# Stick-breaking attention in a Conformer block: the third part's turns behind the next scores, the output's low part in place, the last pair's turns and some out-weight splits further back

## The chip, the cores and the metric

One Trainium2 chip (trn2), one of its cores. The metric is the device time of one execution in microseconds (us), as the median of several. The engines are named as in the profile: PE is TensorE (PEld its weight loads), DVE is VectorE, ACT is ScalarE, POOL is GpSimd, SP is SyncE, which here only issues DMAs. Each engine works through its own queue in order; an instruction that waits holds everything behind it on that engine.

## The reference

One Conformer layer on 1024 frames of width 1024, in float32:

```
x = x + 0.5 * swiglu(rms_norm(x, n1), wi1, wo1)
x = x + stick_breaking_attention(rms_norm(x, mix_norm), w_qkv, q_gain, k_gain, w_o)
x = x + 0.5 * swiglu(rms_norm(x, n2), wi2, wo2)
```

The attention has 16 heads of 64. With z = q.k/8 and strictly earlier frames s < t, the weight of frame s for frame t is sigmoid(z[t,s]) times the product of sigmoid(-z[t,j]) over the frames j between them. The values are summed with these weights, and the heads' outputs go through w_o.

## The kernel before

Every float32 product is made of three products of a high and a low part (`fp32r`): high by high, high by low, low by high. Making the two parts of a tile is called a **split** (`split`, lines 195 to 197): ACT copies the high part, then DVE or POOL subtracts it to get the low part. The kernel runs the first feed-forward block, the attention, the out-projection with w_o, and the second feed-forward block. The change lies in the attention and the out-projection alone.

**The attention** goes through eight pairs of heads, p = 0 to 7. A pair has four parts, a, b, c and d, with lengths in a plan's own units (`PARTS`, line 39). In each part three kinds of work are interleaved:

- *scores* of one head and one half of the frames (`UNITS`, line 41; function `scores`, from line 1038). For a block of 128 frames PE multiplies q and k into a bank `bz` (line 1058; three such banks), ACT takes two sigmoids of it (line 1062, into a tile `w` and back into the bank), DVE runs the product along the row (line 1066, into `om` or `w`), and POOL multiplies the two (line 1073, after a memset of one column, line 1071). The result is a row of attention weights in `w`. Head h and block i have the tile `w{h}{i}`, so `w03` is the last block of head 0.
- *turns and products with the values* of scores made a part earlier (`BEFORE`, line 42; function `values`, from line 1077). A *turn* is up to four transposes of 128x128 by PE into a bank `bt` (line 1095; two such banks), split into `th` and `tl` by ACT and DVE (line 1098). A *product* multiplies `th` and then `tl` into the bank `bo` (line 1113, called `apply` in the code). After the last product of a head ACT and DVE add the outcome to a tile `o` (lines 1118 and 1119), and after the second head of the pair `o` is itself split. For all pairs but the last the two parts went to the tiles `w12` and `w13`, and from there by DMA to DRAM (`o_keep`, lines 1120 to 1127); `load_o` (line 1134) brings them back into `xh` and `xl` for the out-projection. The last pair's parts are written to `xh` and `xl` directly.
- *fills*: the products of the next pair's q, k and v (lines 308 to 310 into the banks `bq`, 24 steps a pair, of six or nine matmuls of 128x384). With the last of a half come sums of squares on ACT and DVE (`sq`, `ssq`), then a chain of small DVE operations for an inverse root (lines 207 to 212), then the scaling of k on POOL (lines 996 and 999). `rs_a` on ACT (line 207) is the first link of that chain and waits for `ssq` (DVE, line 986).

**What sets the order.** Each step is put into a plan at a time in the plan's units: scores evenly over the part, fills evenly, the turns of a part from `TURN` = 4.0 on, and each product `APPLY` = 2.3 after its turn (lines 1187 to 1202). The steps are then emitted in the order of these times (line 1231), and a scheduler under the language reorders single instructions by priority and by what it thinks is ready. So each engine's order is fixed when the kernel is built. `sooner(n)` (line 153) raises the priority of what is emitted in it by n places, and `following(mark)` (line 192) lets an instruction be issued only after a marked one.

**The out-projection.** `out_weights` (line 1245) loads two of the eight row blocks of w_o for one half of the columns, and splits them: high part on ACT, low part on DVE, or on POOL if the name stands in `ON_POOL` (line 35). The first half's four pieces are split during pairs 6 and 7 (low parts: three on POOL, the fourth, tiles `wb` and `wc`, on DVE). The second half's first two pieces (`we`, `wf` and `wg`, `wh`) are split by ACT and DVE during the last pair, and its last two afterwards. As the last pair has no following pair, its fills are replaced by the out-projection's products for the first half of the columns (`SHARES`, line 49; `project`, line 1260), which need 128x512 matmuls of lines 308 to 310 with `raw`, `wa` to `wd` as weights.

Of the kernel before, what the change touches and what calls it, by code (L numbers as in the profile page):

```python
# [17 lines left out]
P = 128  # L18
T = 1024
# [12 lines left out]

BANKS = {"bz": 3, "bq": 2, "bt": 2, "bo": 1, "ka": 2, "kc": 2, "kb": 4, "ma": 4, "mb": 4}

ON_POOL = {"wo0", "wo1", "wo2"}

# [16 lines left out]
)  # L53

TURN, APPLY = 4.0, 2.3
RAW = 6
RH = 4
H_TILES = 8
# [55 lines left out]
def macaron_kernel(ctx, tc, x, g1, w1_in, w1_out, gm, w_qkv, gq, gk, w_o, g2, w2_in, w2_out, out):  # L114
# [801 lines left out]
    with ExitStack() as stack:  # L916
# [121 lines left out]
        def scores(state, hd, half):  # L1038

            w = state["w", hd, half] = {}  # L1040

            def step(tb, kb):
                L = T - tb * P
                if kb == half:
                    t = pl["w"].tile([P, T - tb % 4 * P], F32, name=f"w{hd}{tb % 4}", bufs=1)

                    om = t[:, L : 2 * L] if half else pl["om"].tile([P, T], F32, name="om")
                    state["om"], w[tb] = om, t[:, :L]
                om, wt = state["om"], w[tb]
                q = state["q", hd, half][:, (tb % 4) * P : (tb % 4 + 1) * P]  # L1050
                s0 = max(tb * P, kb * NHALF)
                n = (kb + 1) * NHALF - s0
                c0 = s0 - tb * P
                off = P if n == P else 0
                z = bank("bz")
                keys = slice(s0 - off - kb * NHALF, NHALF)
                for i in range(2):
                    pe.matmul(z[:, : off + n], q, state["k", hd, kb][i][:, keys], start=i == 0, stop=i == 1)  # L1058

                z = z[:, off : off + n]  # L1060
                for to, sign in ((wt[:, c0 : c0 + n], 0), (z, 1)):
                    marks["scored"] = act.activation(  # L1062
                        to, z, AF.Sigmoid, scale=state["f", half][:, sign, tb % 4, hd : hd + 1]
                    ).ins
                least = first[:, P : P + 1].to_broadcast([P, n]) if c0 else first[:, :n]
                dve.tensor_tensor_scan(  # L1066
                    om[:, c0 : c0 + n], z, least, initial=om[:, c0 - 1 : c0] if c0 else 0.0,
                    op0=ALU.mult, op1=ALU.max,
                )
                if c0 == 0:  # L1070
                    pool_e.memset(wt[:, 0:1], 0.0)
                c1 = max(c0, 1)
                pool_e.tensor_tensor(wt[:, c1 : c0 + n], wt[:, c1 : c0 + n], om[:, c1 - 1 : c0 + n - 1], op=ALU.mult)  # L1073

            return [partial(step, tb, kb) for tb in range(half * 4, half * 4 + 4) for kb in range(half, 2)]

        def values(state, p, hd, half):

            own, other = slice(hd * DH, (hd + 1) * DH), slice((1 - hd) * DH, (2 - hd) * DH)
            tb0 = half * 4  # L1080
            now = {}

            def blocks(sb):
                return min(4, sb - tb0 + 1)

            def turn(sbs):
                w = state["w", hd, half]
                tp = bank("bt")
                n = 0
                for sb in sbs:  # L1090
                    for i in range(max(blocks(sb), 2)):
                        c = (sb - tb0 - i) * P

                        src = w[tb0 + i][:, c : c + P] if i < blocks(sb) else first[:, P : 2 * P]
                        pe.transpose(tp[:, n : n + P], src, ident)
                        n += P
                th, tl = now[sbs] = [pl["th"].tile([P, NHALF], F32R, name=n) for n in ("th", "tl")]
                split(tp[:, :n], th[:, :n], tl[:, :n])

            def apply(sbs):  # L1100
                if hd == 0 and sbs[0] == NT - 1:
                    state["o", half] = pl["o"].tile([P, NHALF], F32, name=f"o{half}", bufs=1)
                if sbs[0] == NT - 1:
                    now["o"] = bank("bo")
                ot = now["o"]
                c = 0
                ts = now.pop(sbs)
                for sb in sbs:
                    n = max(blocks(sb), 2) * P
                    vv = state["v"][:, sb, 2 * hd : 2 * hd + 2, :].rearrange("p a b -> p (a b)")  # L1110
                    for i, t in enumerate(ts):
                        start, stop = sb == NT - 1 and i == 0, sb == tb0 and i == 1
                        pe.matmul(ot[:, :n], vv, t[:, c : c + n], start=start, stop=stop)  # L1113
                    c += n
                if sbs[-1] > tb0:
                    return
                o = state["o", half]
                act.activation(o[own, :], ot[other, :], AF.Copy)
                dve.tensor_tensor(o[own, :], ot[own, :], o[own, :], op=ALU.add)
                if hd == 1 and p < NP - 1:  # L1120

                    oh, ol = (
                        pl["w"].tile([P, T - i * P], F32R, name=f"w1{i}", bufs=1)[:, :NHALF] for i in (2, 3)
                    )
                    split(o, oh, ol)
                    for to, src in zip(o_keep, (oh, ol)):
                        sp.dma_start(to[rows(p), HALVES[half]], src.bitcast(F32))
                elif hd == 1:
                    split(o, xh[:, p, HALVES[half]], xl[:, p, HALVES[half]])

            groups = [(sb,) for sb in range(NT - 1, tb0 + 1, -1)] + [(tb0 + 1, tb0)]
            return [(partial(turn, sbs), partial(apply, sbs)) for sbs in groups]

        def load_o(half):

            for i in range(NP - 1):
                for to, src in zip((xh, xl), o_keep):
                    sp.dma_start(to[:, i, HALVES[half]].bitcast(F32), src[rows(i), HALVES[half]])


        states = [{} for _ in range(NP)]
        plan = []
# [34 lines left out]
        for p in range(-1, NP):  # L1177
# [9 lines left out]
            for part, span in PARTS.items():  # L1187
# [3 lines left out]
                if this is not None:  # L1191
                    groups = values(this, p, *BEFORE[part])
                    for i, (to_turn, to_apply) in enumerate(groups):
                        t = TURN + (span - TURN) * i / len(groups)
                        put(part, t, to_turn)
                        put(part, t + APPLY, to_apply)
            if nxt is not None:
                if p >= 0:
                    fills = qkv(p + 1, nxt)
                    for part, span in PARTS.items():  # L1200
                        for i in range(FILLS[part]):
                            put(part, (span - (3.0 if part == "d" else 0.0)) * (i + 0.5) / FILLS[part], fills.pop(0))
                put("c", 15.0, partial(prep_q, nxt, 1))
                put("c", 17.5 if p >= 0 else 20.0, partial(prep_k, nxt, 0, 1))
                put("d", 8.0, partial(prep_k, nxt, 1, 1))
# [35 lines left out]
    with pools(*PROJECTION) as pl:  # L1241
# [3 lines left out]
        def out_weights(c, k, rooms):  # L1245
# [7 lines left out]
            if c is HALVES[0] and k < 6:  # L1253

                there = seen[:, k // 2 : k // 2 + 1] if k < 4 else wo[-1][1][:, 0:1].bitcast(F32)
                pool_e.tensor_tensor((l_ if k < 4 else h_)[:, 0:1], there, there, op=ALU.mult)
            split(raw, h_, l_, lane(f"wo{k // 2}") if c is HALVES[0] else dve)
            return [(h_[:, s], l_[:, s]) for s in HALVES]

        def project(tb, ks, h, tags):  # L1260
# [106 lines left out]
```

## Time and profile before

| what | value |
| --- | --- |
| median of 3 runs | 1930.62 us (1930.38 to 1931.1) |
| profiled execution: its own time | 1931.22 us |
| profiled execution: span of its instructions | 1929.4 us |
| PE busy | 1906.1 us (99%) |
| DVE, POOL, ACT busy | 1237.0 us (64%), 1115.7 us (58%), 978.5 us (51%) |
| attention and the first half of the out-projection | about 667 to 1238 us of the span |

The profile shows one execution. A row of a timeline has the start in us from the span's first instruction, the length in us, the engine, the line, the operation, the tiles (out<-in), the shape and a count of merged neighbours. In brackets stands how long the engine had been idle and what ended that. Matmuls overlap: the next one starts before the one before has ended, so the cost of a matmul in a row of them is the distance from start to start. A wait is therefore a little longer than the idle time in brackets. The view of waits adds this idle time up by who waited for whom.

### The profile page before, as it was taken

Reading aid. Unit: us, or ns where it says so; the run is one execution under the profiler, and the core shown is the slowest. Engines: PE = TensorE matmul, PEld = TensorE weight load, DVE = VectorE, ACT = ScalarE, POOL = GpSimd, SP = SyncE. Lnnn points to the kernel's source line nnn. Section 1 sums busy time; section 2 is a strip of 40 time slices with the busy share of each in tenths; the row PEclk is TensorE's granted clock in tenths of the full one; section 3 lists DMA queues with packets and bytes.
Section 4 is the critical chain, followed back from the end, with each engine's and each line's share of the span. In section 5 each row is a group of like instructions: output and inputs, shape, how many; then the busy total and the mean of one; then the engine's idle time right before and its main releaser. Section 6 shows DMA issues by size and latency. Waiting matters only on the chain.

```text
span 1929.4 us, 26653 instructions
## 1 busy us (share of the span) xinstructions
PE 1906.1 (99%) x9362; PEld 1623.1 (84%) x9362; DVE 1237.0 (64%) x1714; ACT 978.5 (51%) x1794; POOL 1115.7 (58%) x994
## 2 busy tenths in 40 slices
PE   9999999999999999999999999999999999999999
PEld 8878888888888899898989897788888888888887
DVE  6855455536775667887787778477455545548645
ACT  6433433343335467777787777344433443334332
POOL 5766667656456646655665564114667667655554
PEclk9999999999999999999999999999999999999999
DMA  6233323238996401111101144511323323369973
GB/s 202 88 120 105 104 87 126 94 118 294 347 321 234 134 25 45 39 39 45 45 31 48 50 143 141 197 55 59 116 88 125 100 97 104 121 212 341 336 268 139
DMA packets 169558, 259.70 MB, mean 135 GB/s; under 512 B 11728, under 2 KB 82384, under 8 KB 169424
## 3 DMA queue, kind: packets, MB, share of 16 engines
q1 hardware_dynamic: 169280, 258.00, 39.2%
q8 instruction: 73, 1.20, 0.3%
q14 instruction: 61, 0.50, 0.1%
q10 hardware_dynamic: 144, 0.00, 0.0%
HBM read 197.66 MB, written 60.29 MB: 134 GB/s over the span
## 4 chain that ended last, share of the span: by engine, by line
PE 85%; DVE 7%; ACT 2%; POOL 2%; issue 2%; DMA 1%; SPq 0%; DVEq 0%; POOLq 0%; ACTq 0%
PE ka L308 6%; PE ka L310 6%; PE ka L309 6%; PE kc L308 4%; PE kc L310 4%; PE kc L309 4%; PE bq L309 4%; PE bq L308 4%; PE bq L310 4%; PE kb L308 4%; PE ma L309 4%; PE ma L310 4%; PE kb L310 4%; PE ma L308 4%; PE kb L309 4%; PE bo L1113 3%
## 5 line engine op out<-in xcount | busy, mean ns | idle before, releaser
L197 POOL TENSOR_TENSOR rp<-raw,rp 128x1024 fp32r<-128x1024 f32 x84 | 212.5, 2534 | 169.9 <-ACT rp L196 159.1
L197 POOL TENSOR_TENSOR u<-sf,u 128x512 fp32r<-128x512 f32 x160 | 227.4, 1423 | 136.4 <-ACT u L196 136.4
L197 POOL TENSOR_TENSOR u<-raw,u 128x512 fp32r<-128x512 f32 x128 | 186.2, 1457 | 157.9 <-ACT u L196 157.1
L196 ACT ACTIVATE u<-sf 128x512 fp32r<-128x512 f32 x160 | 100.8, 630 | 204.9 <-PE kb L309 86.9
L1073 POOL TENSOR_TENSOR w<-w,om 128x512 f32<-128x512 f32 (+4 forms) x128 | 140.8, 1104 | 110.2 <-DVE om L1066 83.9
L446 DVE TENSOR_TENSOR h<-h 128x512 f32<-128x512 f32 x110 | 135.4, 1235 | 85.7 <-POOL h L554 85.0
L196 ACT ACTIVATE rp<-rh 128x1024 fp32r<-128x1024 f32 (+1 forms) x78 | 76.5, 984 | 196.6 <-PE mb L309 59.2
L308 PE MATMUL bq<-wqh,xh 128*128 128x384 f32 x512 | 174.5, 341 | 0.0
L310 PE MATMUL bq<-wqh,xl 128*128 128x384 f32 x512 | 172.2, 336 | 0.0
L309 PE MATMUL bq<-wql,xh 128*128 128x384 f32 x512 | 172.0, 336 | 0.0
L576 DVE TENSOR_TENSOR raw<-raw 128x1024 f32<-128x1024 f32 (+1 forms) x60 | 89.9, 1500 | 109.8 <-DMA raw<-w_out 94.9
L196 ACT ACTIVATE u<-raw 128x512 fp32r<-128x512 f32 x128 | 80.3, 630 | 151.6 <-PE ka L309 100.9
L308 PE MATMUL ka<-xh,u 128*128 128x512 f32 x352 | 137.2, 390 | 1.9 <-ACT s L499 1.9
L308 PE MATMUL ma<-rp 128*128 128x512 f32 x352 | 137.0, 389 | 0.0
L310 PE MATMUL ka<-xh,u 128*128 128x512 f32 x352 | 137.0, 389 | 0.0
L310 PE MATMUL ma<-rp 128*128 128x512 f32 x352 | 136.9, 389 | 0.0
L309 PE MATMUL ka<-xl,u 128*128 128x512 f32 x352 | 136.9, 389 | 0.0
L309 PE MATMUL ma<-rp 128*128 128x512 f32 x352 | 136.9, 389 | 0.0
L1062 ACT ACTIVATE w<-bz,f 128x512 f32<-128x512 f32 (+2 forms) x192 | 112.7, 587 | 42.2 <-PE bz L1058 39.4
L554 POOL TENSOR_TENSOR h<-h,g 128x512 f32<-128x512 f32 x80 | 112.9, 1411 | 35.4 <-DVE h L503 33.6
L475 DVE TENSOR_TENSOR sf<-raw 128x512 f32<-128x512 f32 x80 | 80.3, 1003 | 77.9 <-POOL u L197 77.9
L197 DVE TENSOR_TENSOR rp<-rh,rp 128x1024 fp32r<-128x1024 f32 (+1 forms) x70 | 110.8, 1600 | 22.1 <-ACT rp L196 19.6
(309 smaller groups left out, 5497.1 us busy)
## 6 DMA issues: line engine op xcount, KB each, us to landing
raw<-w_out SPq DMA_DIRECT2D x120, 512.0 KB, 5.7
raw<-w_in SPq DMA_DIRECT2D x86, 512.0 KB, 3.6
k<-h SPq DMA_DIRECT2D x154, 256.0 KB, 2.1
rh<-k SPq DMA_DIRECT2D x64, 512.0 KB, 6.3
raw_qkv<-w_qkv SPq DMA_DIRECT2D x64, 192.0 KB, 3.0
x_keep<-x SPq DMA_DIRECT2D x32, 256.0 KB, 3.7
x<-x_keep SPq DMA_DIRECT2D x32, 256.0 KB, 5.4
raw<-w_out SPq DMA_DIRECT2D x24, 256.0 KB, 3.6
```

The source lines that it names most:

```text
L196: first = act.activation(hi, raw, AF.Copy).ins
L197: return first, (engine or dve).tensor_tensor(lo, raw, hi.bitcast(F32), op=ALU.subtract).ins
L308: pe.matmul(dst, ah, bh, start=start and i == 0, stop=False, skip_group_check=onto)
L309: pe.matmul(dst, ah, bl, start=False, stop=False, skip_group_check=onto)
L310: pe.matmul(dst, al, bh, start=False, stop=stop and i == n - 1, skip_group_check=onto)
L446: dve.tensor_tensor(src, hb[of[0]], hb[of[1]], op=getattr(ALU, of[2]))
L475: dve.tensor_tensor(f[n], x, y, op=op)
L554: pool_e.tensor_tensor(h, h, gs[k], op=ALU.mult)
L576: dve.tensor_tensor(w[0], w[0], w[1], op=getattr(ALU, W_OF[m][2]))
L1062: marks["scored"] = act.activation(to, z, AF.Sigmoid, scale=state["f", half][:, sign, tb % 4, hd : hd + 1]).ins
L1073: pool_e.tensor_tensor(wt[:, c1 : c0 + n], wt[:, c1 : c0 + n], om[:, c1 - 1 : c0 + n - 1], op=ALU.mult)
L1113: pe.matmul(ot[:, :n], vv, t[:, c : c + n], start=start, stop=stop)
```

## The change

Five edits. First, the turns of part c start at 6.6 of the plan's units instead of 4.0, and are spread over what is left of the part; the last of the four fills in part a is put 0.1 units earlier. Second, the low part of `o` is written over `o` itself, and only the high part goes to a `w` tile (`w13`); the second half of pair 6's output (`half` 0) is written to `xh` and `xl` directly, like that of pair 7. Third, in the last pair the turns and products of parts c and d are emitted with a priority 12 places lower. Fourth, the fourth piece of the first half of w_o has its low part made on POOL. Fifth, the second half's first two pieces have their high parts made after the last score's sigmoid, and their low parts on POOL after the last weighing; all low parts of the second half are made in two steps of 128x512.

```diff
-ON_POOL = {"wo0", "wo1", "wo2"}
+ON_POOL = {"wo0", "wo1", "wo2", "wo3"}
...
-TURN, APPLY = 4.0, 2.3
+TURN, APPLY = {"a": 4.0, "b": 4.0, "c": 6.6, "d": 4.0}, 2.3
...
-                if hd == 1 and p < NP - 1:
-
-                    oh, ol = (
-                        pl["w"].tile([P, T - i * P], F32R, name=f"w1{i}", bufs=1)[:, :NHALF] for i in (2, 3)
-                    )
+                if hd == 1 and (p < NP - 2 or p == NP - 2 and half):
+
+                    oh = pl["w"].tile([P, T - 3 * P], F32R, name="w13", bufs=1)[:, :NHALF]
+                    ol = o.bitcast(F32R)
                     split(o, oh, ol)
...
-            for i in range(NP - 1):
+            for i in range(NP - 2 + half):
...
+        def behind(f, n=12):
+
+            with sooner(-n):
+                f()
...
-                        t = TURN + (span - TURN) * i / len(groups)
+                        t = TURN[part] + (span - TURN[part]) * i / len(groups)
+                        if p == NP - 1 and part in "cd":
+                            to_turn, to_apply = partial(behind, to_turn), partial(behind, to_apply)
...
-                            put(part, (span - (3.0 if part == "d" else 0.0)) * (i + 0.5) / FILLS[part], fills.pop(0))
+                            t = (span - (3.0 if part == "d" else 0.0)) * (i + 0.5) / FILLS[part]
+                            put(part, t - 0.1 if (part, i) == ("a", FILLS["a"] - 1) else t, fills.pop(0))
...
-            split(raw, h_, l_, lane(f"wo{k // 2}") if c is HALVES[0] else dve)
+            if c is HALVES[0]:
+                split(raw, h_, l_, lane(f"wo{k // 2}"))
+            else:
+                with following(marks["scored"] if k < 4 else None):
+                    act.activation(h_, raw, AF.Copy)
+                with following(marks["weighed"] if k < 4 else None):
+                    for s in HALVES:
+                        engine = pool_e if k < 4 else dve
+                        engine.tensor_tensor(l_[:, s], raw[:, s], h_[:, s].bitcast(F32), op=ALU.subtract)
```

What this does to the engines' orders is shown at three places.

PE in part c of the second pair, before. `w_7487`, `w_7534`, `w_7572` and `w_7630` are the tiles `w00` to `w03`; the two `bz` rows are the score of the second block of head 1:

```order
L310 MATMUL bq<-wqh,xl 128x384
L1095 MATMUL bt<-ident,w_7487 128x128
L1095 MATMUL bt<-ident,w_7534 128x128
L1095 MATMUL bt<-ident,w_7572 128x128
L1095 MATMUL bt<-ident,w_7630 128x128
...
L1058 MATMUL bz<-kh_s_7582,q_s_7406 128x384
L1058 MATMUL bz<-kl_s_7583,q_s_7406 128x384
L308 MATMUL bq<-wqh,xh 128x384
```

The same place now (`w_7485`, `w_7532`, `w_7570` and `w_7628` are the same four tiles):

```order
L1097 MATMUL bt<-ident,w_7628 128x128
L1058 MATMUL bz<-kh_s_7206,q_s_7404 128x512
L1115 MATMUL bo<-th,vst 128x512
L1058 MATMUL bz<-kl_s_7207,q_s_7404 128x512
L308 MATMUL bq<-wqh,xh 128x384
L309 MATMUL bq<-wql,xh 128x384
L310 MATMUL bq<-wqh,xl 128x384
L1115 MATMUL bo<-tl,vst 128x512
```

Two turns of four transposes each stood ahead of the score of 128x384 and nine fill matmuls, and now stand behind them; the first product with `th` (line 1113 before, 1115 now) follows the turns after one score matmul, where there were a score and four fill matmuls between.

ACT at the same place, now (before, the row with `th` stood between `vst` and `rs_a`, and the two rows with 128x384 behind `rs_a`):

```order
L984 ACTIVATE vst<-bq 128x2x64
L1062 ACTIVATE w_7725<-bz,f_7303 128x384
L1062 ACTIVATE bz<-bz,f_7303 128x384
L207 ACTIVATE rs_a<-ssq 128x16
L196 ACTIVATE th<-bt 128x512 x2
```

So the high parts of the two turns now stand behind `rs_a` on ACT.

DVE at the end of pair 6's part d, before (`w_12296` is a score block of head 0 of the last pair):

```order
L197 TENSOR_TENSOR tl<-bt,th 128x512
L197 TENSOR_TENSOR wc<-raw,wb 128x1024
L1066 SCALAR_TENSOR_TENSOR w_12296<-bz,first 128x256
L197 TENSOR_TENSOR tl<-bt,th 128x512
L986 TENSOR_REDUCE ssq<-sq 128x4
```

POOL there, now (`w_12221` and `w_12283` are the blocks `w01` and `w02` of that head):

```order
L1073 TENSOR_TENSOR w_12221<-w_12221 128x383
L197 TENSOR_TENSOR wd<-raw,wa 128x1024
L197 TENSOR_TENSOR wc<-raw,wb 128x1024
L1071 MEMSET w_12283 128x1
L1073 TENSOR_TENSOR w_12283<-w_12283 128x255
```

The low part `wc` has left DVE's queue ahead of a score and a `tl`, and stands in POOL's between `wd` and the weighing of `w02`.

More of the change, by code (lines that the diff above doesn't have):

```diff
@@ L1072, in step @@
                 c1 = max(c0, 1)
-                pool_e.tensor_tensor(wt[:, c1 : c0 + n], wt[:, c1 : c0 + n], om[:, c1 - 1 : c0 + n - 1], op=ALU.mult)
+                marks["weighed"] = pool_e.tensor_tensor(
+                    wt[:, c1 : c0 + n], wt[:, c1 : c0 + n], om[:, c1 - 1 : c0 + n - 1], op=ALU.mult
+                ).ins
             return [partial(step, tb, kb) for tb in range(half * 4, half * 4 + 4) for kb in range(half, 2)]
```

## The prediction

> **What bounds the kernel now.** First the page's busy times, then the view of windows by stage, then the waits of PE in the first seven pairs (720 to 1147 us) and in the last one (1147 to 1240 us).
>
> ```profile
> PE 1906.1 (99%) x9362; PEld 1623.1 (84%) x9362; DVE 1237.0 (64%) x1714; ACT 978.5 (51%) x1794; POOL 1115.7 (58%) x994
> 797.00:862.00 65.00, 63.97 (x389) 1.00 0.13 40
> 1148.00:1240.00 92.00, 86.93 (x448) 1.00 0.46 151
> PE bt L1095 <- POOL w L1071: 4.4, 7, 0.6
> PE bz L1058 <- DVE w L1066: 1.7, 5, 1.1
> PE bo L1113 <- DVE tl L197: 1.7, 6, 0.3
> ...
> PE bo L1113 <- DVE tl L197: 1.3, 2, 0.9
> PE bt L1095 <- POOL w L1073: 1.2, 1, 1.2
> PE bt L1095 <- ACT bz L1062: 0.8, 1, 0.8
> PE bz L1058 <- DVE rs_u L211: 0.4, 1, 0.4
> PE bz L1016 <- POOL qk L996: 0.4, 1, 0.4
> PE bt L1095 <- POOL w L1071: 0.3, 1, 0.3
> ```
>
> PE is the bound, and none of its matmuls is removed or added: the change can only win or lose waits. A middle pair's 65 us hold 1.0 us of them; the last pair's 92 us hold 5.1. So some 13 us are all there is, a little more as a stop costs more than the idle time it shows (1.02 us against 0.86 in an example below).
>
> **Third part's turns, seven pairs.** This is part c of the second pair, on PE, POOL, DVE and ACT:
>
> ```profile
> 797.11 0.49 PE L1095 MATMUL bt<-ident,w 128*128 128x128 f32 x3
> 798.20 0.76 PE L1095 MATMUL bt<-ident,w 128*128 128x128 f32 x5 [0.61 <-POOL w L1071]
> 798.72 0.42 PE L1058 MATMUL bz<-kh_s,q_s 128*128 128x384 f32 x1
> 796.51 1.63 POOL L1073 TENSOR_TENSOR w<-w,om 128x512 f32<-128x512 f32 x1 [3.10 <-DVE om L1066]
> 799.64 0.41 DVE L986 TENSOR_REDUCE ssq<-sq 128x4 f32<-128x256 f32 x1
> 798.63 1.08 ACT L196 ACTIVATE th<-bt 128x512 fp32r<-128x512 f32 x2
> 800.08 0.22 ACT L207 ACTIVATE rs_a<-ssq 128x16 f32<-128x16 f32 x1 [0.37 <-DVE ssq L986]
> 800.21 0.56 ACT L1062 ACTIVATE w<-bz,f 128x384 f32<-128x384 f32 x1
> ```
>
> The fourth transpose needs `w03`, which POOL has ready at 796.51 + 1.63 = 798.14 (the memset behind it is only named because it ends at the same moment). Eight transposes take 1.61 us here (797.11 to 798.72); where nothing waits, four take 0.36 (774.68 to 775.04 in the rows of the next part). So 0.8 us are lost, seven times 5.6.
>
> Now the turns stand behind the score (two matmuls, of which the row at 798.72 shows one; 0.4 together, an estimate from it) and nine fill matmuls (1.60, 776.21 to 777.81 below): they begin at 797.11 + 0.4 + 1.6 = 799.1, a microsecond after `w03` is there. That wait goes.
>
> What is late next is the first product, which needs `th`. PE comes to it after eight transposes (0.8) and one score matmul (0.3, my estimate from the rows' spacing), at 800.2. Before, ACT made both `th` from 798.63 on, ahead of `rs_a`; now they stand behind it, and `rs_a` waits for DVE's `ssq`, done at 799.64 + 0.41 = 800.05, since DVE works through a run of scans that PE's order doesn't hasten. `rs_a` starts at 800.08, the next operation at 800.21, and one `th` of the two takes about 0.6: ready at 800.8. **PE waits 0.65 us at the product instead of 0.8 at the turn: 0.15 a pair, seven pairs, 1.1 us.** Bounds: 5.6 gained if `th` costs no wait at all; 5.6 lost if a scan of about 0.95 us comes ahead of `ssq` on DVE (a wait of 1.6). I take the value worked out from the rows.
>
> **The last fill of part a ahead of a score.** These are the rows around the begin of part b:
>
> ```profile
> 774.68 0.49 PE L1095 MATMUL bt<-ident,w 128*128 128x128 f32 x3
> 775.04 0.42 PE L1113 MATMUL bo<-th,vst 128*128 128x384 f32 x1
> 775.87 0.38 PE L1058 MATMUL bz<-kh_s,q_s 128*128 128x256 f32 x1 [0.16 <-DVE w L1066]
> 776.21 0.34 PE L308 MATMUL bq<-wqh,xh 128*128 128x384 f32 x1
> 777.81 0.28 PE L1113 MATMUL bo<-th,vst 128*128 128x256 f32 x1
> 778.56 0.39 PE L1113 MATMUL bo<-tl,vst 128*128 128x256 f32 x1 [0.24 <-DVE tl L197]
> 777.83 0.68 DVE L197 TENSOR_TENSOR tl<-bt,th 128x512 fp32r<-128x512 f32 x1
> ```
>
> The score no longer waits 0.16 for its bank, as nine fill matmuls now run first. But the product at 778.56 waits for a `tl` that DVE ends at 778.51 out of a run without gaps; PE gets there earlier and waits as much longer. I count **nothing**; at most the two waits, 0.4 a pair, 2.8 us, if DVE comes earlier too.
>
> **The output's low part in place.** One pair differs from the others at this place:
>
> ```profile
> 905.59 0.47 ACT L1062 ACTIVATE w<-bz,f 128x256 f32<-128x256 f32 x1 [1.76 <-DMA o_keeph<-w]
> 909.05 0.37 ACT L1062 ACTIVATE w<-bz,f 128x128 f32<-128x128 f32 x1
> ```
>
> ACT waits there 1.76 us for the store of `w12`, and PE behind it 1.1 (the longest in the second row of waits) instead of some 0.15. Now only `w13` holds a stored part, and ACT asks for it 3.5 us later (909.05). **0.9 us go**; the range is 0 to 0.9, as a later landing in another execution is not shown. The stores and loads of pair 6's second half go from SP's queue too; no wait of PE is theirs.
>
> **The low part on POOL, and the later splits, last pair.** The rows are DVE's and POOL's at the end of pair 6 and PE's wait there, then two other such splits on DVE:
>
> ```profile
> 1154.90 2.40 POOL L197 TENSOR_TENSOR wd<-raw,wa 128x1024 fp32r<-128x1024 f32 x1 [1.56 <-issue]
> 1156.08 2.31 DVE L197 TENSOR_TENSOR wc<-raw,wb 128x1024 fp32r<-128x1024 f32 x1 [0.77 <-ACT wb L196]
> 1158.91 0.66 DVE L197 TENSOR_TENSOR tl<-bt,th 128x512 fp32r<-128x512 f32 x1
> 1158.28 0.48 PE L1113 MATMUL bo<-th,vst 128*128 128x512 f32 x1
> 1159.62 0.51 PE L1113 MATMUL bo<-tl,vst 128*128 128x512 f32 x1 [0.86 <-DVE tl L197]
> 1159.07 0.72 POOL L1073 TENSOR_TENSOR w<-w 128x255 f32<-128x255 f32 x1 [1.73 <-DVE w L1066]
> 1172.62 1.21 DVE L197 TENSOR_TENSOR wf<-raw,we 128x1024 fp32r<-128x1024 f32 x1
> 1192.74 1.95 DVE L197 TENSOR_TENSOR wh<-raw,wg 128x1024 fp32r<-128x1024 f32 x1
> ```
>
> `wc` holds DVE for 2.31 us ahead of the `tl` for which PE waits: from 1158.28 to 1159.62 are 1.34 us where such a pair takes 0.32, so 1.02 are lost. With `wc` gone from DVE, `tl` is there by 1158.4, and the wait is gone. On POOL `wc` follows `wd` at 1157.3 and ends at 1159.7; the weighing queued behind it (1159.07 before) starts 0.7 us late, and the turn that reads it comes at 1161 at the earliest. Cover 0.5: nothing lost; 0.5 if the cover is short. **1.0 gained.** The waits on `rs_u` and `qk` just after stand behind ACT and DVE queues that move by the same microsecond as PE: they stay, 1.2 us with their restarts.
>
> Of two pages of the Trainium skill one speaks against this edit: GPSIMD Engine Reference, section 4.1, puts a two-input elementwise operation on GpSimd at about twice VectorE's time, and 2.40 against the 1.21 of a DVE split agrees. By that rule alone the edit would cost 1.2 us instead of winning 1.0. SBUF — State Buffer, section "Who interferes with whom", says that a VectorE operation with two SBUF inputs contends with a reading GpSimd one; the 2.31 us of `wc`, beside `wd`, agree.
>
> **The last pair's parts b to d.** Of its waits, those of 0.84 (on `bz`), 0.3, 0.5 (the second row with `tl`) and 1.23, with the smaller ones 3.4 us of idle time and with eight restarts 4.9 us, lie where the order changes.
>
> ```profile
> 1215.67 0.33 PE L1095 MATMUL bt<-ident,w 128*128 128x128 f32 x1 [1.23 <-POOL w L1073]
> 1174.17 0.39 PE L308 MATMUL bq<-raw,xh 128*128 128x512 f32 x1
> 1174.40 0.39 PE L309 MATMUL bq<-raw,xh 128*128 128x512 f32 x1
> ```
>
> The wait of 1.23 goes: between the last score and the turn that reads it now stand 18 out-projection matmuls (0.23 each, 1174.17 to 1174.40), four transposes and eight products, over 5 us of PE's work, and the chain of two sigmoids, scan and weighing takes about 4 (an estimate: the weighing 1.6 at most by its row above, the scan and the sigmoids not much more than 1.2 each). The one on `tl` goes with `wh` (1.95 us on DVE). In exchange the turns and products of part d close up at the end: about 1.0 us after a turn (two products and three transposes) PE wants a `tl`, which takes 0.6 on ACT, 0.66 on DVE and some 0.3 of hand-over: about 0.6 lost. And part b's scores, freed of turns between them, come closer: six to eight times, by their places in the order, a `bz` bank or a weighed tile will not be ready, as a scan of 128x512 is longer than the PE work in between. I put these at 0.15 to 0.45 each, 2.0 us in all, an estimate. **4.9 - 0.6 - 2.0 = 2.3 gained**; bounds 4.3 and -0.5. POOL's four late steps (2 x 2.4 by the row of `wd`) end by about 1221 (the last weighing ends with the wait at 1215.67), and the out-projection of the second half, which needs them, begins over 10 us after that, behind all turns and products: covered.
>
> **Sum.** 1.1 + 0 + 0.9 + 1.0 + 2.3 = 5.3 us. The profiled execution took 1931.22 (span 1929.4), 0.6 over the median; its one wait of 0.9 may be that excess, so I take off 0.2 less: 5.1 from the median, 1930.62 - 5.1 = **1925.5 us**.
>
> **Rivals.**
> 1. *`th` is in time* (ACT's idle 0.37 before `rs_a` speaks for slack; the order, with `rs_a` first, against): all 5.6 of part c are won, 1930.62 - 5.6 - 4.0 = 1921.0. Chance 0.14.
> 2. *The last pair's waits only move*: DVE is as full as before and the banks fill up; 1.1 + 0.9 remain of the sum, 1928.6. For it: DVE runs without gaps for stretches there; against: three splits leave it. Chance 0.25.
> 3. *The new wait at the first product is longer than the old one.* ACT and DVE are queues; each 0.1 us by which `ssq` is later costs 0.7 over seven pairs. At a wait of 1.4 the 4.2 us of the other terms are eaten up, at 1.95 the kernel is 3.9 us slower, 1934.5. For it: the bound of 1.6 above; against: DVE's order there keeps `ssq` ahead of the scan. Chance 0.10.
> 4. *No edit does anything*, since every wait is bound by DVE's run and turns up elsewhere: 1930.6. Chance 0.05.
>
> My forecast has the remaining 0.46, and some 1.5 us either way.
>
> **How the numbers follow.** 0.2% are 3.9 us, about what a measurement of this kernel tells from no change: the line is at 1926.8. Of the forecast's 0.46 lie 0.06 above the line; the rest and rival 1 give faster 0.54. Rivals 2 and 4, that 0.06 and half of rival 3 (a wait of 1.4 is no change) give 0.41 for within 0.2%, and its other half slower 0.05. The range leaves out the far side of rival 1 (its upper bounds together) and rivals 3 and 4: 1920.0 to 1929.5.
>
> **What would show it.** In the profile of the changed kernel: no wait of a turn on POOL in part c, and in its place a wait of about 0.5 on ACT's `th` at the first product, seven times; the wait on `tl` at the begin of part b 0.3 longer; no `wc` on DVE and no wait near 1158; none of 1.2 near the last turns. If `th` shows no wait, rival 1 is right; if PE's idle time in the last pair's 92 us stays near 5, rival 2.

## The result, and the profile after

| | before | changed |
| --- | --- | --- |
| median | 1931.16 us (6 runs, 1930.38 to 1932.11) | 1922.72 us (6 runs, 1922.49 to 1923.53) |
| profiled execution: its own time, span | 1931.22, 1929.4 us | 1922.76, 1920.9 us |

The ratio is 0.9957, 95% interval 0.9944 to 0.997: 8.4 us faster, where 5.3 were forecast (5.1 off the median of the three runs shown). The direction and the range held (forecast 1925.5, range 1920.0 to 1929.5); the size was too small by 3 us. This is the page's row of busy times and, from the view of windows, a middle pair (part c of the second pair lies in it) and the last pair's stretch, both moved by what the changed kernel is ahead there. The columns are window, length, PE busy, PEld, DVE, ACT, POOL, granted clock, DMA share and GB/s.

```profile
PE 1900.9 (99%) x9362; PEld 1624.1 (85%) x9362; DVE 1234.6 (64%) x1713; ACT 980.5 (51%) x1794; POOL 1126.3 (59%) x999
795.00:860.00 65.00, 63.76 (x392) 59.61 (x391) 52.26 (x102) 51.69 (x114) 38.66 (x59) 1.00 0.14 43
1142.00:1232.00 90.00, 87.45 (x455) 70.23 (x454) 61.25 (x98) 54.60 (x105) 40.10 (x51) 1.00 0.46 152
```

The last pair's idle time fell from 5.07 us in 92 to 2.55 in 90. The middle pair's grew, from 1.03 to 1.24 us in 65, although it got faster: the same 65 us now hold 392 matmuls instead of 389. The page's busy time of PE fell from 1906.1 to 1900.9 us with 9362 matmuls as before, so busy time itself was won. Some waits do not show as idle time, and this is where the forecast missed most.

PE's waits in the first seven pairs (720 to 1144 us) and in the last one (1144 to 1232), from the view of waits (the idle time in total, how many waits, the longest):

```profile
PE bo L1115 <- ACT th L196: 3.9, 7, 0.6
PE bo L1115 <- DVE tl L197: 3.7, 6, 0.7
```

```profile
PE bz L1058 <- DVE om L1066: 1.0, 3, 0.4
PE bz L1058 <- DVE rs_u L211: 0.5, 1, 0.5
PE bz L1016 <- POOL qk L996: 0.4, 1, 0.4
PE bo L1115 <- DVE tl L197: 0.2, 1, 0.2
PE bt L1097 <- POOL w L1073: 0.2, 1, 0.2
```

Seven waits on POOL's `w` (4.4 us) became seven on ACT's `th` (3.9), those on `tl` at the begin of part b grew from 1.7 to 3.7, those on `bz` banks (1.7, of which 1.1 near 907 us) are gone, and of the last pair's long waits (1.23, 0.86, 0.84, 0.5) none is left.

The exchange in part c of the second pair, on PE, DVE and ACT:

```profile
797.31 1.04 PE L1097 MATMUL bt<-ident,w 128*128 128x128 f32 x8
797.94 0.41 DVE L986 TENSOR_REDUCE ssq<-sq 128x4 f32<-128x256 f32 x1
798.11 0.48 PE L1058 MATMUL bz<-kh_s,q_s 128*128 128x512 f32 x1
798.38 0.22 ACT L207 ACTIVATE rs_a<-ssq 128x16 f32<-128x16 f32 x1 [0.47 <-DVE ssq L986]
798.50 1.07 ACT L196 ACTIVATE th<-bt 128x512 fp32r<-128x512 f32 x2
799.13 0.50 PE L1115 MATMUL bo<-th,vst 128*128 128x512 f32 x1 [0.55 <-ACT th L196]
```

The eight transposes run without a stop. ACT makes `th` from 798.50, behind `rs_a`, which waited 0.47 us for `ssq`, as the prediction had it. PE starts the product 1.02 us after the score's matmul. Such a matmul behind transposes takes 0.31 from start to start where nothing waits (in the kernel both_later below):

```profile
799.24 0.48 PE L1058 MATMUL bz<-kh_s,q_s 128*128 128x512 f32 x1
799.55 0.39 PE L1058 MATMUL bz<-kl_s,q_s 128*128 128x512 f32 x1
```

So 0.7 us are lost here.

**Where the 8.4 us lie.** Both kernels run 9362 matmuls, and at equal numbers the same stage has been reached. So the time between two numbered matmuls can be set against the same in the other trace. I cut the stretch from the 3051st to the 6551st, the attention, into: seven pieces of 150 matmuls around part c's turns (from the 3387th, 388 apart); the six pieces that lie between those; the end of pair 6 (5865th to 5951st); the last pair (5951st to 6401st). What is left of the stretch is the same in all kernels within 0.1 us, and from the 6551st to the end it is 635.3 in both. Each row is one profiled execution:

| kernel | part c, 7 pieces | between, 6 pieces | end of pair 6 | last pair | whole stretch |
| --- | --- | --- | --- | --- | --- |
| before | 179.2 | 239.4 | 14.9 | 95.9 | 617.0 |
| changed | 176.6 | 238.1 | 14.05 | 93.6 | 609.9 |
| control (before again) | 179.3 | 239.6 | 14.8 | 95.8 | 617.2 |
| c_turn | 176.6 | 240.1 | 15.0 | 95.1 | 614.4 |
| c_turn_near | 180.7 | 241.4 | 14.9 | 95.9 | 620.6 |
| c_apply | 176.5 | 240.0 | 15.0 | 94.9 | 614.0 |
| low | 179.4 | 237.9 | 14.8 | 96.9 | 616.7 |
| wo3 | 179.3 | 239.2 | 13.9 | 96.0 | 616.1 |
| last_pair | 179.3 | 239.6 | 14.9 | 93.8 | 615.1 |
| behind_only | 179.5 | 239.6 | 14.9 | 93.9 | 615.6 |
| late_only | 179.4 | 239.9 | 14.9 | 97.2 | 619.0 |
| root_after_turns | 177.2 | 238.0 | 14.0 | 93.5 | 610.3 |
| product_a_later | 176.7 | 235.7 | 14.0 | 93.5 | 607.5 |
| both_later | 173.1 | 235.7 | 14.0 | 93.5 | 604.1 |

The changed kernel wins 2.6 in part c, 1.3 between (1.24 of it in the one piece with the store's wait), 0.85 at the end of pair 6 and 2.3 in the last pair: 7.1. Another 1.3 us it was ahead already at the 3051st matmul (671.34 against 672.63), where no engine works in another order yet.

### The profile page after: what moved, and what is told of

Its sections match the earlier page's. It is cut to its first block, busy times and chain, and to the rows that moved or that the text cites. A ratio compares the mean times of both kernels' runs of the same rounds, so it can differ in the third digit from the quotient of the medians.

```text
span 1920.9 us, 26652 instructions
## 1 busy us (share of the span) xinstructions
PE 1900.9 (99%) x9362; PEld 1624.1 (85%) x9362; DVE 1234.6 (64%) x1713; ACT 980.5 (51%) x1794; POOL 1126.3 (59%) x999
## 4 chain that ended last, share of the span: by engine, by line
PE 90%; DVE 5%; ACT 2%; POOL 1%; issue 1%; DMA 1%; DVEq 0%; ACTq 0%; POOLq 0%
PE ka L308 6%; PE ka L310 6%; PE ka L309 6%; PE bq L310 5%; PE bq L308 5%; PE bq L309 5%; PE kc L310 4%; PE kc L308 4%; PE kc L309 4%; PE bo L1115 4%; PE ma L309 4%; PE ma L308 4%; PE ma L310 4%; PE kb L310 4%; PE kb L308 4%; PE kb L309 4%
## 5 line engine op out<-in xcount | busy, mean ns | idle before, releaser
L576 DVE TENSOR_TENSOR raw<-raw 128x1024 f32<-128x1024 f32 (+1 forms) x60 | 96.1, 1604 | 106.3 <-DMA raw<-w_out 96.2
L1062 ACT ACTIVATE w<-bz,f 128x512 f32<-128x512 f32 (+1 forms) x192 | 113.4, 591 | 50.9 <-PE bz L1058 47.2
```

Source lines behind the costliest of these rows:

```text
L576: dve.tensor_tensor(w[0], w[0], w[1], op=getattr(ALU, W_OF[m][2]))
L1062: marks["scored"] = act.activation(to, z, AF.Sigmoid, scale=state["f", half][:, sign, tb % 4, hd : hd + 1]).ins
```

## The experiments

Every kernel below was timed against the kernel before on the same chip. The letters in the expectations stand for the theory (A) and its rival (B).

**The kernel before, again** (no edit).

> The kernel before, once more, for a second profile. Theory S (the 1.3 us by which the changed kernel's profile is ahead before the first attention score are chance: landings of weights in the first feed-forward block): this execution reaches the same matmul (number 3100, 680.91 us before) within a microsecond to either side of 680.9. Rival C (the change moves that time): 680.9 again within 0.2. In the attention, equal matmuls keep their distance within 0.1 us but for the one wait on the DMA near 905 us, which shows again with 1.6 to 2.4 us.

1930.75 us against 1930.85 (ratio 0.9999, 0.999 to 1.0008). The 3101st matmul came at 680.92 us, 0.01 from before. By this run alone rival C stands. But the order of every engine is the same in all kernels of this study up to about 710 us, and the 3051st matmul came between 671.3 and 672.6 us in the profiles at full clock: at 671.34, 671.57 and 672.35 in three kernels that hold all five edits, at 671.55 to 672.47 in four whose first difference lies behind 1150 us. In the attention the pieces repeat within 0.1 us but for the store's wait, which is there again, on ACT:

```profile
905.88 0.47 ACT L1062 ACTIVATE w<-bz,f 128x256 f32<-128x256 f32 x1 [1.97 <-DMA o_keeph<-w]
```

So a piece can be compared to about 0.1 us from one profile each. The time ahead of the attention scatters by more than a microsecond, without a pattern that follows the edits.

**The first edit alone, and the place of the products alone.** In c_turn the turns begin at 6.6 and products stay 2.3 behind; in c_turn_near they stand 1.9 behind; in c_apply nothing is changed but 2.3 to 2.6 in part c.

```diff
 c_turn, c_turn_near:
-TURN, APPLY = 4.0, 2.3
+TURN, APPLY = {"a": 4.0, "b": 4.0, "c": 6.6, "d": 4.0}, 2.3
...
 c_turn_near besides:
-                        put(part, t + APPLY, to_apply)
+                        put(part, t + (1.9 if part == "c" else APPLY), to_apply)
 c_apply alone:
-                        put(part, t + APPLY, to_apply)
+                        put(part, t + (2.6 if part == "c" else APPLY), to_apply)
```

> Only the first edit: turns of part c from 6.6 on, the last fill of part a 0.1 earlier. The prediction's step gives 1.1 us (0.15 in each of seven pairs). Theory A, read from the two traces: 0.42 in each of seven pairs, 3.0 us, since each product of part c now also stands behind the next turn (turns 2.06 units apart, products 2.3 behind their own), so that the small waits on th and tl go as well; a wait of about 0.55 idle on ACT's th stays at the first product. Rival B: the surplus over 0.15 comes from the other edits (tiles of other pools, DVE and POOL less loaded), then this kernel gains about 1.1 us alone.

> Only one number: in part c the products stand 2.6 units behind their turns instead of 2.3, so that they come behind the next turn (turns stay 2.43 units apart, from 4.0 on). Theory A: the wait of 0.6 on POOL at the fourth turn stays in each of seven pairs, and the small waits at the products go: about 0.3 a pair, 2 us faster. Rival B: no gain, within 0.5 us of before.

> The first edit alone (turns of part c from 6.6 on), but the products of part c 1.9 units behind their turns instead of 2.3, so ahead of the next turn (turns 2.06 apart) as before the change. Theory A (of the 0.42 a pair most came from the products' place behind the next turn): about 0.1 a pair or nothing is left of it, and small waits on th and tl at the products of part c show again. Rival B (it came from the turns' later begin): 0.4 a pair, as with the first edit whole.

c_turn: 1928.32 us against 1931.14 (ratio 0.9985, 0.9976 to 0.9994). c_apply: 1927.37 against 1931.14 (0.9982, 0.9973 to 0.999). c_turn_near: 1932.38 against 1931.5 (1.0007, 0.9998 to 1.0017). A piece of part c takes 25.6 us before, 25.2 in c_turn, 25.2 in c_apply and 25.8 in c_turn_near: theory A in all three. (The later products also win 0.8 and 1.0 us in the last pair, in c_turn and c_apply.) These are PE's waits in the first seven pairs of c_turn and then of c_apply:

```profile
PE bo L1113 <- ACT th L196: 5.5, 8, 1.5
PE bo L1113 <- DVE tl L197: 2.5, 6, 0.5
```

```profile
PE bt L1095 <- POOL w L1071: 4.4, 7, 0.6
PE bz L1058 <- DVE w L1066: 2.1, 5, 1.5
PE bo L1113 <- DVE tl L197: 1.7, 6, 0.3
```

c_apply keeps all seven waits on POOL, 0.6 each, and wins as much in part c as the changed kernel. c_turn_near moves the turns and wins nothing, it loses 0.2 a pair. That loss is not the exchange of waits alone: the same exchange stands in c_turn with the same steps, and 1.9 units also bring one product nearer to its own turn than before (1.3 us behind the turn's begin instead of 2.8). It comes 0.42 us after the begin of two transposes, which take 0.22 where nothing waits, and its row is 0.50 long:

```profile
809.75 0.38 PE L1095 MATMUL bt<-ident,w 128*128 128x128 f32 x2
810.17 0.50 PE L1113 MATMUL bo<-th,vst 128*128 128x512 f32 x1
```

So what the first edit gains comes from the products' place, as c_apply shows, and not from the wait that it takes off the turns. Turns 2.43 units apart with products 2.3 behind put each product just ahead of the next turn; at 2.06 apart it stands behind the next turn, and its `th` and `tl` have four transposes more of time. These are later products of part c on PE, before and then changed:

```profile
806.39 0.40 PE L1113 MATMUL bo<-th,vst 128*128 128x512 f32 x1
806.74 0.50 PE L1113 MATMUL bo<-tl,vst 128*128 128x512 f32 x1
807.07 0.60 PE L1095 MATMUL bt<-ident,w 128*128 128x128 f32 x4
```

```profile
801.54 0.60 PE L1097 MATMUL bt<-ident,w 128*128 128x128 f32 x4
801.89 0.48 PE L1115 MATMUL bo<-th,vst 128*128 128x512 f32 x1
802.21 0.39 PE L1115 MATMUL bo<-tl,vst 128*128 128x512 f32 x1
...
803.74 0.60 PE L1097 MATMUL bt<-ident,w 128*128 128x128 f32 x4
804.09 0.48 PE L1115 MATMUL bo<-th,vst 128*128 128x512 f32 x1
804.41 0.39 PE L1115 MATMUL bo<-tl,vst 128*128 128x512 f32 x1
```

Before, the `tl` product starts 0.35 us after the `th` product and the next instruction 0.33 after that, where such a matmul has 0.23; its row is 0.50 long instead of 0.39, and no bracket shows idle time. A wait this short shows in the lengths of rows only. In the changed kernel the `tl` row is back to 0.39. (The 0.32 from 801.89 to 802.21 is no wait: four transposes and the matmul behind them take 0.67 from 801.54 to 802.21, and 0.67 also where the next such group stands, from 803.74 to 804.41.)

With the tile `w12` still stored by DMA, c_turn keeps the store's wait, 2.40 us on ACT, and its pieces between take 0.7 us more than before. Most of that is the scatter of this wait: late_only (below), whose orders are those of before up to 1166 us, has 2.42 there and takes 0.4 more. Whether the first edit makes the store's wait longer is not shown. The row of late_only:

```profile
905.93 0.47 ACT L1062 ACTIVATE w<-bz,f 128x256 f32<-128x256 f32 x1 [2.42 <-DMA o_keeph<-w]
```

**The low part in place, alone** (the second edit's lines of the diff).

> Only the low part in place and pair 6's second half written directly. Theory A, as in the prediction: the one wait of 1.76 us on ACT for the store of the low part goes, 0.9 us faster, all of it in that one pair. Rival B: the store's landing varies from one execution to the next, the wait of before was chance, and nothing is gained; then another wait on a DMA can show in this kernel too.

1929.76 us against 1931.14 (0.9994, 0.9986 to 1.0003; by the interval this can't be told from no change). The store's wait is gone, and the piece that had it is 1.25 us shorter (39.54 against 40.79, with its neighbours at 39.5 to 39.6): theory A at this place, and more than its 0.9. In the eight profiles of kernels that store `w12` with a full clock there the wait is always there, and the piece is 1.1 to 1.8 us longer than its neighbours, 1.5 on average. The rest was not foreseen: alone, this edit makes the last pair 1.0 us slower, so that the whole stretch is only 0.4 shorter. The last pair's work is emitted in another order there, and a product waits longer for `tl`:

```profile
PE bo L1113 <- DVE tl L197: 2.4, 3, 1.4
```

With the other edits nothing is left of that wait.

**The low part on POOL, alone** (`ON_POOL` with `"wo3"`).

> Only the fourth low part of the first half of w_o on POOL instead of DVE. Theory A, as in the prediction: the wait of 0.86 on tl near 1159 goes and none comes in its place, 1.0 us faster (0.8 by the two traces). Rival B: POOL's weighing behind it is late by more than its cover and the turn that reads it waits: 0 to 0.5 us gained.

1929.83 us against 1931.14 (0.9995, 0.9987 to 1.0004; by the interval this can't be told from no change). The end of pair 6 is 1.0 us shorter, and nothing comes in its place in the last pair (+0.1): theory A. POOL there in the changed kernel:

```profile
1149.81 2.40 POOL L197 TENSOR_TENSOR wd<-raw,wa 128x1024 fp32r<-128x1024 f32 x1 [1.64 <-issue]
1152.16 2.40 POOL L197 TENSOR_TENSOR wc<-raw,wb 128x1024 fp32r<-128x1024 f32 x1
1154.55 0.75 POOL L1073 TENSOR_TENSOR w<-w 128x255 f32<-128x255 f32 x1
```

**The last pair's edits, together and apart** (the third edit, `behind`, and the fifth, the later splits).

> Only the third and the fifth edit: turns and products of the last pair's parts c and d 12 places further back, and the late splits of the second half's out-weights. Theory A, as in the prediction: the waits of 0.84, 0.5 and 1.23 go, smaller ones on bz banks come, 2.3 us faster, all of it between 1165 and 1240 us; the DMA wait near 905 and the wait of 0.86 near 1159 stay. Rival B: alone it loses what the first edit's later turns bring to the last pair (the first edit alone gained 0.7 there), and 1.5 remain.

> Only the third edit, the turns and products of the last pair's parts c and d 12 places further back. Theory A: the waits at turns (0.84 on ACT's bz, 1.23 on POOL's w) go, the one on tl behind the split wh on DVE stays: 1.0 to 1.5 us of the 1.9 that both edits won together. Rival B: without the later splits DVE holds tl and om, and nothing is won.

> Only the fifth edit, the late splits of the second half's out-weights. Theory A: the wait of 0.5 on tl behind wh (and small ones) goes, the 0.84 and the 1.23 at the turns stay: 0.4 to 0.9 us. Rival B: DVE, freed of two splits (1.2 and 1.95 us), also makes the turns' inputs earlier, and most of the 1.9 us comes from this edit alone.

last_pair: 1928.39 us against 1930.85 (0.9988, 0.9979 to 0.9997). behind_only: 1929.62 against 1931.5 (0.999, 0.998 to 0.9999). late_only: 1931.15 against 1931.5 (1.0, 0.9991 to 1.0009). The last pair takes 93.8, 93.9 and 97.2 us, where it took 95.9. The third edit alone is worth 2.0 and the fifth nothing that can be measured; with the turns further back, the wait on `tl` behind `wh` is gone without an edit of that split (what is left at that product in behind_only is 0.04 us). So behind_only wins more than theory A's 1.0 to 1.5, and late_only less than its 0.4 to 0.9. The wait of 0.84 that theory A had going stays, with 0.94 in behind_only, and here in last_pair:

```profile
1177.28 0.78 PE L1097 MATMUL bt<-ident,w 128*128 128x128 f32 x2 [0.84 <-POOL w L1071]
```

In low it is gone: there the second edit changed the order. The third and fifth edits take off idle time of 0.3, 0.5 and 1.23 and bring in last_pair 0.2 on a `bz` bank and 0.1 on `tl`. late_only's 97.2 is too long by a lower clock in this one execution, as its windows show (the granted clock is the third column from the right); in the other profiles that stretch has 1.00:

```profile
1165.00:1180.00 15.00, 13.35 (x63) 9.90 (x62) 12.04 (x22) 9.51 (x19) 7.49 (x12) 0.96 0.72 236
1180.00:1196.00 16.00, 15.52 (x73) 12.03 (x72) 12.54 (x16) 11.21 (x22) 9.58 (x13) 0.93 0.00 1
```

**`th` ahead of `rs_a` again.** The changed kernel, with the chain behind `ssq` made a step of its own, behind the first two turns of part c.

```diff
-                y = rsqrt(pl["sq"], ssq.rearrange("p a b -> p (a b)"), 1.0 / DH, room[:, :16])
...
+                if half and p:
+                    state["root"] = partial(norm_qk, half, room, ssq)
...
+                with following(marks["turned"] if half and p else None):
+                    y = rsqrt(pl["sq"], ssq.rearrange("p a b -> p (a b)"), 1.0 / DH, room[:, :16])
...
-                split(tp[:, :n], th[:, :n], tl[:, :n])
+                marks["turned"] = split(tp[:, :n], th[:, :n], tl[:, :n])[0]
...
+                if p >= 0:
+                    put("c", 8.7, lambda s=nxt: s["root"]())
```

> The changed kernel, in which rs_a of part c (line 207) may only issue after the high parts of the first two turns, so that th stands ahead of it on ACT again. Theory A (th waits because it stands behind rs_a, and that behind ssq): the wait of 0.55 on th at the first product shrinks to about 0.15 in each of seven pairs, 3.5 to 4.2 us faster than the changed kernel (1922.7), about 1919. Rival B (th is bound by the transposes themselves, or the chain behind rs_a is then late and another wait takes its place): less than 1 us.

1923.42 us against 1930.85 (0.9962, 0.9949 to 0.9976), so no faster than the changed kernel; a piece of part c takes 25.30, 0.08 more. Rival B holds, though the first half of theory A is right. The rows of the second pair:

```profile
798.31 0.41 DVE L986 TENSOR_REDUCE ssq<-sq 128x4 f32<-128x256 f32 x1
798.38 1.09 ACT L196 ACTIVATE th<-bt 128x512 fp32r<-128x512 f32 x2
798.48 0.48 PE L1066 MATMUL bz<-kh_s,q_s 128*128 128x512 f32 x1
798.64 0.95 DVE L1074 TENSOR_TENSOR_SCAN om<-bz,first 128x384 f32<-128x384 f32 x1
799.03 0.50 PE L1123 MATMUL bo<-th,vst 128*128 128x512 f32 x1
799.50 1.26 DVE L197 TENSOR_TENSOR tl<-bt,th 128x512 fp32r<-128x512 f32 x2
800.22 0.50 PE L1123 MATMUL bo<-tl,vst 128*128 128x512 f32 x1
```

The `th` product comes 0.55 us after the score's matmul instead of 1.02 (798.11 to 799.13 in the changed kernel), 0.47 earlier. But `tl` stands behind the 0.95 us of a scan on DVE, and PE then stops at the `tl` product instead. One wait had hidden the other.

**Products further back.** The changed kernel with the last product of part a behind a score and nine fill matmuls of part b, and then the first product of part c as well.

```diff
 product_a_later:
-                        put(part, t + APPLY, to_apply)
+                        put(part, t + (3.3 if part == "a" and i == len(groups) - 1 else APPLY), to_apply)
 both_later, in place of the same line:
+                        far = {("a", len(groups) - 1): 3.3, ("c", 0): 2.7}
+                        put(part, t + far.get((part, i), APPLY), to_apply)
```

> The changed kernel with the last product of part a 3.3 units behind its turn instead of 2.3, so that a score and nine fill matmuls of part b (some 2 us) come ahead of it. Theory A (the wait of 0.7 on tl is only a matter of distance): it goes in each of six or seven pairs, 4 to 4.9 us faster than the changed kernel, about 1918. Rival B (DVE's run sets the pace there): the score's bank bz or the next turn waits instead, less than 1 us.

> The changed kernel with the last product of part a 3.3 units behind its turn and the first product of part c 2.7 behind its own (all others 2.3), so that this first product comes behind nine fill matmuls (1.6 us). Theory A (the waits left at these products are a matter of distance alone): the wait on th in part c, 0.7 to 0.8 from start to start, goes in each of seven or eight pairs, 5 to 6 us faster than with part a's product alone (1921.3), about 1916, and no wait on th is left in part c. Rival B (DVE's run sets the pace, as it did when rs_a was moved behind the turns): a tl or a bank further on waits instead, 1920 to 1921.

product_a_later: 1921.26 us against 1930.85 (0.9948, 0.9936 to 0.9961); both_later: 1918.2 against 1931.5 (0.9932, 0.9919 to 0.9946), the fastest kernel of the study, 13 us ahead of the one before and some 4.5 of the changed one. The first wins 0.4 us in each of six pairs (the pieces between the parts c went from 39.55 to 39.13), half of what was expected, since a wait of 0.2 on `kl_s` shows up. The second wins 0.5 a pair in part c (25.24 to 24.73), of the 0.7 to 0.8 expected. The rest shows up a few products further on, in the lengths of rows: the `th` product takes 0.37 and the `tl` product 0.34 from start to start, where the changed kernel's took 0.32 and 0.23, and the matmuls behind them lose 0.2 more:

```profile
804.37 0.47 PE L1115 MATMUL bo<-th,vst 128*128 128x512 f32 x1
804.74 0.50 PE L1115 MATMUL bo<-tl,vst 128*128 128x512 f32 x1
```

PE's waits in the first seven pairs of both_later:

```profile
PE bz L1058 <- DVE kl_s L1021: 1.0, 5, 0.2
PE bo L1115 <- DVE tl L197: 0.5, 2, 0.3
```

No idle time on `th` is left. Theory A is right on the place and the sign; it put the size half as high again as it is (0.7 to 0.8 a pair for 0.5), and rival B's `tl` is where the rest went.

## Why the prediction was right or wrong

- **Part c's turns, 1.1 forecast, 2.6 measured: the sign right by luck, the cause wrong.** The exchange of waits came as written (no wait on POOL at a turn; seven of 0.55 on `th` at the first product, about 0.5 having been named). But it wins nothing, where 0.15 a pair was forecast: some 0.8 was lost before (1.61 for eight transposes that take 0.80 now) and 0.8 is lost now (0.7 ahead of the product, and 0.1 as the next matmul comes 0.33 after it instead of 0.23). c_turn_near, which makes this exchange and keeps the products ahead of the next turn, wins nothing either. The step that failed is the list of effects: that the closer turns put every product behind the next turn was not on it, and it is worth 0.4 to 0.6 a pair by c_apply and by c_turn against c_turn_near. It could have been read ahead of time from the start-to-start distances of the product rows (0.35 and 0.33 for 0.23), where the views of idle time show nothing. Rival 1, `th` in time, did not occur; its time was near the result for another reason. Rival 3's longer wait did not come either: the new one costs what the old one did, far from the break-even of 1.4.
- **The ceiling of some 13 us was wrong too.** It was added up from idle time, and both_later won 12.9 us in the stretch (617.0 to 604.1) with 3.8 us of idle time left in the two lists of its waits (1.5 in the first seven pairs, 2.3 in the last).
- **Last fill of part a, nothing forecast: right.** The wait on `tl` grew from 0.28 to 0.62 a pair, those on `bz` went, and the pieces between the parts c take 39.55 instead of 39.58.
- **Low part in place, 0.9 forecast, 1.24 measured: mechanism right, size low.** I priced PE's longest wait less a usual one; the piece as a whole shows 1.2, in the control 1.4, and 1.5 on average of the eight profiles. Taking 0.2 off for chance was wrong as well: the wait is there in every profile with `w12` stored.
- **Low part on POOL, 1.0 forecast, 0.85 measured (1.0 alone): right.** No row of DVE has `wc`, no wait near 1154 is left, and the waits on `rs_u` and `qk` stayed, 0.5 and 0.4. On the rule of GPSIMD Engine Reference, section 4.1, in the Trainium skill, which speaks against the edit, the trace agrees in the price (2.40 on POOL, 1.21 on an undisturbed DVE), but the price fell on an engine with time to spare. On SBUF — State Buffer, "Who interferes with whom", the runs agree too: `wd` takes 2.40 on POOL with and without a split on DVE beside it, and it was DVE's that took 2.31.
- **Last pair, 2.3 forecast, 2.3 measured: right in size, in part by luck, and half right in cause.** The 1.23 went, the new small waits came (five on `bz`, `w` and `tl` in the list above, beside the two that stayed), the end's wait on `tl` is 0.23 idle. But the wait on `tl` went with the turns, not with `wh`: behind_only wins 2.0 of it and the later splits nothing measurable. And the 0.84 went with the second edit, not with these. The new waits, 2.6 in the sum, came to some 0.3 of idle time in last_pair and 1.1 in the changed kernel. So the 4.9 to be won and the 2.6 to be lost were both too high, and their difference came out. Rival 2 fell with the idle time of 2.55 us.
- **The remaining 1.3 us stay open.** The profiles differ by that much ahead of the attention, and so do the medians from the stages' sum (8.4 against 7.1). In the profiles some 0.6 of it arises in the first 18 matmuls (last section), and some 0.7 near 647 us, where PE's transposes of line 287 wait for `x` of DVE. These are the waits between 640 and 660 us, before and changed; c_turn, wo3 and root_after_turns show the shorter form too, the other kernels the longer one:

```profile
PE mb L287 <- DVE x L622: 1.4, 3, 0.5
PE mb L287 <- DVE x L622: 0.9, 2, 0.5
```

Two profiles of the kernel before agree at the 3051st matmul to 0.01 us; those of the others, with the same orders up to there, scatter from 671.3 to 672.6 us. Whether the medians' 1.3 are chance or something of the build that no view shows was not told apart; 0.3 of it may be the store's wait, which the profile of before shows 0.3 shorter than the average.

## What to carry to other kernels

When PE is the bound and hardly idle, add up start-to-start distances of like matmuls as well as idle time, and compare two traces at equal matmul numbers: waits of a tenth of a microsecond, many times, show in no view of idle time, only in the lengths of rows. Whoever moves one kind of step in an interleaved plan should ask what it now stands before and behind: here the distance of a product from its turn was worth more than the wait that the move was made for. Here a wait on a chain of two engines (`th` on ACT, `tl` on DVE) went when its consumer moved back behind both (both_later); an earlier first link alone showed the wait on the second (root_after_turns).

## What the runs showed of the hardware

The kernel's first matmuls start 0.43 us apart, then 0.23, and how many are slow differs between the profiles, from 6 to 14 (13 and 14 in the two of the kernel before). The first row of PE, 18 matmuls of 128x512, differs by 0.76 us for it, before and then changed:

```profile
1.64 7.18 PE L691 MATMUL kc<-xl 128*128 128x512 f32 x18 [1.64 <-POOL xl L685]
```

```profile
1.64 6.42 PE L691 MATMUL kc<-xl 128*128 128x512 f32 x18 [1.64 <-POOL xl L685]
```

The granted clock (third from the right) reads 1.00 all the same, here in the kernel before, where the slow ones last until 7.4 us:

```profile
4.00:6.00 2.00, 2.00 (x6) 1.59 (x5) 1.03 (x4) 0.89 (x3) 0.45 (x1) 1.00 1.05 365
```

The Trainium skill, TensorE: Matmul & The Clock Gate, Part 1, gives 426.7 and 215.7 ns from start to start for matmuls with 512 columns while the array is cold and once it is warm, and says that the number of cold ones changes from run to run. The rows agree in the first figure (0.427 us) and show 0.227 us, 5% more, for the second; here the measured figure counts. That the number changes between runs of one kernel, the 13 and 14 above show by one matmul only.

In two of the 14 profiles the clock was granted lower for 30 to 45 us in the attention: 0.93 to 0.96 in late_only, and 0.96 in c_turn_near from 895 to 940 us, where the piece with the store's wait took 42.8 us, against 40.7 to 41.4 in the other kernels with that wait.

```profile
895.00:940.00 45.00, 42.61 (x244) 38.72 (x243) 35.72 (x76) 33.08 (x74) 21.85 (x34) 0.96 0.12 39
```
